# Retention in chunks of 64 tokens instead of 128, with all its products in quarters of TensorE's array

## The chip, the cores and the metric

The kernel runs on one core of one Trainium2 chip. The metric is device time in microseconds (us) for one execution; the time given for a kernel is the median over several runs.

## What is computed

One decoder layer on 2048 tokens of width 1024. One input projection of the normalised x (1024 to 2816 columns) feeds two head groups; both results are gated, put side by side and mapped back by an output projection, and x is added. Group B is a sliding-window attention with 8 heads; the change does not touch it. Group A is retention with 4 heads, keys of 64 and values of 128 columns, cut to its core:

```python
qc, kc, vc = chunks(q), chunks(k), chunks(v)              # chunks of C tokens, N = S / C
decay = where(diff >= 0, exp(log_g * diff), 0)            # diff = i - j inside a chunk
scores = einsum('bhnid,bhnjd->bhnij', qc, kc) * decay
intra = einsum('bhnij,bhnje->bhnie', scores, vc)
zeta = exp(log_g * (C - 1 - i))
kv = einsum('bhnjd,bhnje->nbhde', kc * zeta, vc)
state = exp(log_g * C) * state + kv                       # one step for each chunk; prev is the state before it
cross = einsum('bhnid,nbhde->bhnie', qc * xi, prev)       # xi = exp(log_g * (i + 1))
ro = intra + cross                                        # then a norm over each head's 128 columns
```

The result is the same for every length of chunk: a longer chunk has more inside it (`intra`) and fewer steps of the state.

## The kernel before

**The large products.** Four products (query and key columns of the attention, of the retention, gates, output projection) hold most of TensorE's time. Each splits its float32 operands into a high and a low part and multiplies those in three passes (fp32r). Each is made of blocks of 2x2 with seven products instead of eight (`Turns`, `products`). In the profile they are the tile `acc` with 128x512 or 128x384 columns. ScalarE makes the high part of every block `x` and `w`, VectorE the low part; VectorE and ScalarE also take the sums out of PSUM.

**The small products.** Transposes, logits, values and retention write PSUM banks, all named `m` in the profile. Logits (`m<-ks,qT`) use the array in eighths (64 rows by 32 columns), the values' products halves and quarters.

**Retention** (`retention`, lines 860 to 1040). It walks over 16 chunks `c` of 128 tokens. For each chunk the DMA queue loads `a` (queries and keys) and `v`; VectorE applies the rotation and makes `qk`; ScalarE scales the keys (line 920); `qk` is transposed by DMA to `qkT`. TensorE then makes, in plain fp32 (two records in the profile for each matmul):

- the scores of all four heads, in quarters of 64x64, and behind them, into the same two banks `pros`, the part of the state (lines 946 to 967; `m<-qkT`, `m<-state,qkT`). The bank is chosen by the half of the array's rows: `pros[i]` with rows `halves[i]`;
- the outputs from the decayed scores `sT` and `v`, in the whole 128x128 array (lines 977 to 989; `m<-v,sT`);
- the update `pkv` from `qk` and `v`, in halves of 128x64 (lines 993 to 1001; `m<-v,qk`).

VectorE multiplies the scores by the decay mask `dm` (two instructions of 128x256 a chunk, line 968) and steps the state (two of 128x128 a chunk, line 1009). ScalarE copies the outputs to `ro` (line 1029). After each four chunks a group norm runs: some twenty small VectorE instructions, 16 normalisations on ScalarE, and stores of `ro` to DRAM, one of 256 KB for each chunk (line 1077). The gate stage loads it back as `go` (line 1403), multiplies by SiLU of the gate and turns it for the output projection: even chunks by DMA, odd chunks on TensorE (`m<-ident,go`).

**What sets the order.** Nothing is ordered by hand. Every operation is put into `Program` with a cost for each engine, what it reads and writes, and a due time in units of large products; `emit` (line 169) then writes one fixed order for each engine. It counts a change of the array's shape on TensorE (`CUTS`, `CHANGE`, line 90) and holds back shapes that would change it. Buffers come from pools: 93 of 2 KB a partition (`k`), 6 half ones (`h`, for `sT` and the state), 8 PSUM banks, of which the small products may hold six (`SHARE`, `rest`). Each engine runs its instructions in this order, so one that waits holds up all behind it. All DMAs but one are issued by the SP queue.

Of the kernel before, what the change touches and what calls it, by code (L numbers as in the profile page):

```python
# [29 lines left out]
F32 = mybir.dt.float32  # L30
# [26 lines left out]
CAP = {"k": 93, "h": 6, "bank": 8}  # L57
# [334 lines left out]
def layer(ctx, tc, xt, xfirst, xtok, nw, w_in, w_rn, qkw, sinks, biasg, rope, decays, dmask, gpow, w_out, out):  # L392
# [40 lines left out]
    def given(ap):  # L433
        return Buf(ap=ap)
# [48 lines left out]
    rsq_all = fixed([P, NCH], "rsq_all")  # L483
    dec = fixed([P, 2, RH], "dec")
# [15 lines left out]
    ro_dram = scratch([P, 512], "ro_dram", NCH)  # L500
# [359 lines left out]
    def retention(at):  # L860

        for i, (t, r) in enumerate(zip(factors, (rstd_all, rsq_all))):
            op(
                {"V": (0.25, 0.33, True)},
                lambda e, t=t, r=r, i=i: e.tensor_tensor(
                    t(), dec()[:, i : i + 1, :].to_broadcast([P, NCH, RH]),
                    r().unsqueeze(2).to_broadcast([P, NCH, RH]), ALU.mult,
                ),
                [dec, r], [t], at(0) - 6, label="factors",
            )  # L870
        op(
            {"V": (0.25, 0.33, True)}, lambda e: e.tensor_tensor(squares(), factors[0](), factors[0](), ALU.mult),
            [factors[0]], [squares], at(0) - 6, label="factors",
        )
        dm = kb("dm", "ret")
        load(dm, given(dmask.rearrange("p h i -> p (h i)")), at(0) - 4)
        state = None
        st = None
        for c in range(NCH):
            due = at(c)  # L880
            a, v = kb("a", "rin"), kb("v", "rin")
            a0, a1 = (Part(a, lambda t, s=s: t[:, s]) for s in (slice(0, 384), slice(384, 512)))
            v0, v1 = (Part(v, lambda t, s=s: t[:, s]) for s in (slice(0, 256), slice(256, 512)))
            soon = due - (EARLIER_K if c in TURNED["qk"] else 0)
            load(a0, rq_dram[0][c], soon - 3, 192, also=(a,))
            load(a1, rq_dram[1][c], soon - 3, 64, also=(a,), of=lambda t: t[:, 0:128])
            if c % NP == 0:
                phases = kb("phases", "rin")
                load(phases, given(rope[c // NP]), soon - 3)
            load(v0, rq_dram[1][c], due - 3, 128, also=(v,), of=lambda t: t[:, 128:384])  # L890
            load(v1, aq_dram[1][c], due - 3, 128, also=(v,), of=lambda t: t[:, 256:512])

            tcos, tsin, qk = kb("tcos", "ret"), kb("tsin", "ret"), kb("qk", "ret")
            for i, t in enumerate((tcos, tsin)):

                def go(e, t=t, a=a, phases=phases, o=c % NP * 64 + i * 32):
                    h = "p (h f) -> p h f"
                    e.tensor_tensor(
                        t().rearrange(h, f=32), a().rearrange(h, f=32),
                        phases()[:, o : o + 32].unsqueeze(1).to_broadcast([P, 16, 32]), ALU.mult,  # L900
                    )

                op(both(512), go, [a0, a1, phases], [t], soon, label="rotary", also=(a,))

            for i, alu in enumerate((ALU.subtract, ALU.add)):

                def go(e, i=i, alu=alu, tcos=tcos, tsin=tsin, qk=qk):
                    r = "p (h a f) -> p h a f"
                    x, y = (tcos, tsin) if i == 0 else (tsin, tcos)
                    e.tensor_tensor(  # L910
                        qk().rearrange("p (a b f) -> p a b f", b=2, f=32)[:, :, i, :],
                        x().rearrange(r, h=2, f=32)[:, 0],
                        y().rearrange(r, h=2, f=32)[:, 1],
                        alu,
                    )

                op(both(256), go, [tcos, tsin], [qk], soon + 0.1, label="rotary sum")


            def go(e, qk=qk, c=c):  # L920
                for h in range(RH):
                    k = qk()[:, 256 + h * RDK : 256 + (h + 1) * RDK]
                    e.activation(k, k, AF.Copy, scale=factors[1]()[:, c, h : h + 1])

            op({"A": (0.95, 1.05, False)}, go, [qk, factors[1]], [qk], soon + 0.15, label="scale k")

            pt, qkT = ps(), kb("qkT", "ret")

            if c in TURNED["qk"]:
                turn_by_dma(qk, qkT, planes_dram[3][c], soon + 0.1)  # L930
            else:

                def go(e, pt=pt, qk=qk):
                    for i in range(4):
                        e.transpose(pt()[:, i * P : (i + 1) * P], qk()[:, i * P : (i + 1) * P], ident())

                op(turns(4), go, [qk, ident], [pt], due + 0.2, "small", label="turn qk")

                op({"A": act(512)}, lambda e, pt=pt, qkT=qkT: e.activation(qkT(), pt(), AF.Copy), [pt], [qkT], due + 0.3,
                   label="qkT")  # L940
            halves = (slice(0, 64), slice(64, 128))


            pros, sTs = [ps(), ps()], [hb("sT"), hb("sT")]

            def go(e, pros=pros, qkT=qkT, state=state):
                for pr in range(2):
                    for u, q in enumerate(halves):
                        for i, r in enumerate(halves):
                            o = 256 + pr * P  # L950
                            e.matmul(
                                pros[i]()[q, o : o + P], qkT()[r, o + u * 64 : o + u * 64 + 64],
                                qkT()[r, pr * P : (pr + 1) * P], start=True, stop=True,
                            )
                for pr in range(2 if state else 0):
                    for u, q in enumerate(halves):
                        for i, r in enumerate(halves):
                            o = pr * P
                            e.matmul(
                                pros[i]()[q, o : o + P], qkT()[r, o + u * 64 : o + u * 64 + 64], state()[r, o : o + P],  # L960
                                start=(pr == 0), stop=False, skip_group_check=True,
                            )

            op(
                f32(P, 2 if c == 0 else 4), go, [qkT] + ([state] if c else []), pros,
                due + 0.4, "quarters", label="scores",
            )
            for i in range(2):
                op(
                    {"V": dve(256)},  # L970
                    lambda e, sT=sTs[i], pro=pros[i], i=i: e.tensor_tensor(
                        sT(), pro()[:, 256:512], dm()[:, i * 256 : (i + 1) * 256], ALU.mult
                    ),
                    [pros[i], dm], [sTs[i]], due + 0.5, label="decay",
                )

            def go(e, pros=pros, sTs=sTs, v=v, c=c):
                for pr in range(2):
                    for i in range(2):
                        h, s = 2 * pr + i, slice(pr * P, (pr + 1) * P)  # L980
                        e.matmul(
                            pros[i]()[:, s], sTs[i]()[:, s], v()[:, h * P : (h + 1) * P], start=(c == 0 and pr == 0),
                            stop=(pr == 1), skip_group_check=True,
                        )

            op(
                f32(P, 4), go, [*sTs, v0, v1], pros, due + 0.6, "small",
                label="outputs", also=(v,),
            )
            if c < NCH - 1:  # L990
                pkv, new = ps(), hb("state")

                def go(e, pkv=pkv, qk=qk, v=v):
                    for h in range(RH):
                        r = slice((h % 2) * 64, (h % 2) * 64 + 64)
                        e.matmul(
                            pkv()[r, (h // 2) * P : (h // 2 + 1) * P], qk()[:, 256 + h * 64 : 256 + (h + 1) * 64],
                            v()[:, h * P : (h + 1) * P], start=True, stop=True,
                        )

                op(f32(P, 2.5), go, [qk, v0, v1], [pkv], due - 1.0, "columns", label="update", also=(v,))
                if c == 0:
                    op(
                        {"V": dve(256)}, lambda e, new=new, pkv=pkv: e.tensor_copy(new(), pkv()[:, 0:256]),
                        [pkv], [new], due + 0.6, label="state",
                    )
                else:
# [22 lines left out]
            if c % NORMED == 0:  # L1030
                st, ros = sb("st", [P, NORMED, RH, 6]), []
# [582 lines left out]
```

## Time and profile before

| What | Value |
|---|---|
| Time, median of 3 runs | 692.14 us (691.63 to 695.44) |
| Span of the profiled execution | 689.9 us, 2.2 us below that median |
| TensorE busy | 683.8 us, 99% of the span |
| VectorE busy | 602.1 us, 87% |
| ScalarE busy | 474.1 us, 69% |
| GpSimd busy | 46.1 us, 7% |
| Bytes moved by DMA | 179.16 MB, mean 260 GB/s |

The profile is of one execution; its span runs from the first to the last instruction. In it PE is TensorE's matmuls, PEld its weight loads, DVE VectorE, ACT ScalarE, POOL GpSimd, SPq the queue that issues DMAs. A row such as `m<-v,sT 128*128 128x128 f32 x128` reads: written tile, read tiles, part of the array in use (rows*columns), size of the moving operand, type, count. A busy time is a union of records that overlap, so the time of one instruction in a row of equals is read from start to start. All of the kernel's instructions have one line, that of the helper that records them, so tiles tell them apart.

### The profile page before, as it was taken

To read this page: it belongs to the slowest core of one execution; us is meant where nothing else is said; L and a number is where in the kernel's file an instruction comes from. 1 tells how busy PE (TensorE), PEld (TensorE's weight loads), DVE (VectorE), ACT (ScalarE), POOL (GpSimd) and SP (SyncE) were. 2 spreads that over 40 slices of the span, in tenths; PEclk is the share of its full clock that TensorE was granted. 3 is DMA by queue.
4 is the path that set the end of the run, shared out by engine and by line. 5 is a ranking of instruction groups with operands and counts; after the bars stand their busy time and mean duration, and the time that the engine had idled before them with its cause. 6 is when DMAs were issued, how large, how long until landed. Compare 5 with 4: busy or idle time off the path is not lost.

```text
span 689.9 us, 15034 instructions
## 1 busy us (share of the span) xinstructions
PE 683.8 (99%) x5164; PEld 586.9 (85%) x5164; DVE 602.1 (87%) x1467; ACT 474.1 (69%) x1121; POOL 46.1 (7%) x75
## 2 busy tenths in 40 slices
PE   9999999999999999999999999999999999999998
PEld 7888888889999999997888888888888888888886
DVE  6999887777899978998999989997979899998862
ACT  7666974657796766888868989989789944253300
POOL 1000000035011001012101010100000000000000
PEclk9999999999999999999999999999999999999999
DMA  9999964989987799999999989899999998126622
GB/s 324 363 352 313 386 209 167 337 289 286 325 217 198 219 297 283 314 287 282 325 284 251 328 242 292 248 221 340 273 355 316 228 274 229 32 76 208 221 106 92
DMA packets 166717, 179.16 MB, mean 260 GB/s; under 512 B 71152, under 2 KB 99824, under 8 KB 166640
## 3 DMA queue, kind: packets, MB, share of 16 engines
q1 hardware_dynamic: 166496, 178.19, 86.4%
q8 instruction: 41, 0.67, 0.4%
q14 instruction: 36, 0.29, 0.1%
q10 hardware_dynamic: 144, 0.00, 0.0%
HBM read 106.77 MB, written 56.69 MB: 237 GB/s over the span
## 4 chain that ended last, share of the span: by engine, by line
PE 99%; issue 0%; DVE 0%
PE acc L388 84%; PE m L388 15%; DVE t L388 0%; DVE none L388 0%
## 5 line engine op out<-in xcount | busy, mean ns | idle before, releaser
L388 PE MATMUL acc<-w,x 128*128 128x512 f32 (+1 forms) x2700 | 589.9, 377 | 0.0
L388 PEld LDWEIGHTS acc<-w,x 128*128 128x128 f32 x2700 | 493.1, 188 | 79.9 <-issue 2.3
L388 DVE TENSOR_TENSOR x<-x 128x512 fp32r<-128x512 f32 (+2 forms) x220 | 145.3, 683 | 16.6 <-ACT x L388 16.5
L388 ACT ACTIVATE x<-x 128x512 fp32r<-128x512 f32 (+1 forms) x187 | 110.9, 615 | 17.4 <-DVE x L388 11.7
L388 DVE TENSOR_TENSOR w<-w 128x512 fp32r<-128x512 f32 (+3 forms) x96 | 61.7, 659 | 2.7 <-ACT w L388 2.3
L388 ACT ACTIVATE w<-w 128x512 fp32r<-128x512 f32 (+1 forms) x72 | 40.7, 599 | 21.0 <-DVE w L388 10.2
L388 ACT ACTIVATE pm<-lg,nm 128x128 f32<-128x128 f32 x128 | 49.7, 393 | 5.2 <-DVE lg L388 5.1
L388 DVE TENSOR_TENSOR s<-acc,s 128x512 f32<-128x512 f32 (+1 forms) x64 | 41.6, 651 | 10.9 <-PE acc L388 10.3
L388 DVE SCALAR_TENSOR_TENSOR w<-w,nw_sb 128x512 fp32r<-128x512 f32 (+3 forms) x72 | 49.5, 709 | 1.2 <-ACT w L388 1.1
L388 DVE CUSTOM_DVE_ANT_0 lg<-m,bias,nsnk 128x160 f32<-128x160 f32 x128 | 42.4, 379 | 7.6 <-PE m L388 7.5
L388 POOL TENSOR_SCALAR_AFFINE_SELECT own<-pT 64x512 f32<-64x512 f32 x32 | 29.0, 920 | 243.9 <-ACT pT L388 214.2
L388 DVE TENSOR_TENSOR t<-acc,t 128x512 f32<-128x512 f32 (+2 forms) x33 | 21.1, 640 | 17.7 <-PE acc L388 17.1
L388 ACT ACTIVATE x<-go 128x512 fp32r<-128x512 f32 x40 | 24.1, 623 | 13.1 <-PE acc L388 3.5
L388 DVE TENSOR_TENSOR x<-go,x 128x512 fp32r<-128x512 f32 x40 | 27.3, 682 | 2.5 <-ACT x L388 2.5
L388 ACT ACTIVATE apart<-qn 128x1024 uint16<-128x1024 uint16 x16 | 16.9, 1054 | 18.2 <-DVE qn L388 18.1
L388 ACT ACTIVATE w<-w,nw_sb 128x512 fp32r<-128x512 f32 (+3 forms) x43 | 27.5, 677 | 2.6 <-DMA w<-in_w_in 2.6
L388 ACT ACTIVATE s<-acc 128x512 f32<-128x512 f32 (+1 forms) x32 | 18.0, 566 | 14.6 <-PE acc L388 11.7
L388 DVE TENSOR_TENSOR r<-acc,t 128x512 f32<-128x512 f32 (+1 forms) x32 | 20.8, 651 | 7.0 <-PE acc L388 6.7
L388 ACT ACTIVATE ro<-ro,nmu,rg 128x128 f32<-128x128 f32 x64 | 25.1, 481 | 0.4 <-DVE nmu L388 0.4
L388 ACT ACTIVATION_READ_ACCUMULATOR pm<-lg,nm 128x1 f32 x128 | 24.5, 191 | 0.0
L388 ACT ACTIVATE c<-acc 128x512 f32<-128x512 f32 (+1 forms) x24 | 13.3, 560 | 15.1 <-PE acc L388 13.1
L388 PE MATMUL m<-ks,qT 64*32 64x160 f32 x1024 | 22.1, 300 | 1.6 <-issue 1.6
(132 smaller groups left out, 681.7 us busy)
## 6 DMA issues: line engine op xcount, KB each, us to landing
x<-in_xt SPq DMA_DIRECT2D x80, 256.0 KB, 4.8
x<-s_dram SPq DMA_DIRECT2D x64, 256.0 KB, 4.6
planes_dram<-apart SPq DMA_DIRECT2D x56, 256.0 KB, 4.2
w<-in_w_in SPq DMA_DIRECT2D x40, 256.0 KB, 5.4
s_dram<-x SPq DMA_DIRECT2D x32, 256.0 KB, 4.5
xk<-in_xtok SPq DMA_DIRECT2D x32, 256.0 KB, 5.2
res<-in_xtok SPq DMA_DIRECT2D x32, 256.0 KB, 3.8
w<-in_w_out SPq DMA_DIRECT2D x20, 256.0 KB, 5.2
```

Of the source, the lines that this page charges most:

```text
L388: return lambda *a, **k: self.order.put(op(*a, **k))
```

## The change

The chunk of retention becomes 64 tokens. The program takes two old chunks of 128 tokens, four of 64, at a time (`for c in range(0, NCH, 2)`).

- **Update**: eight quarter matmuls for each 128 tokens instead of four in halves, one bank `kvs[u]` for each half `u` of the rows, that is for each chunk of 64 of the two.
- **State**: it is stepped every 64 tokens, 31 times instead of 15; the pool `h` has 8 buffers instead of 6. An update may go only behind the scores of the pair before (`held_up`).
- **State's part, scores, outputs**: state's part goes first, then the scores, 64 columns wide instead of 128, only inside a chunk of 64. Outputs are quarter matmuls as well. A pair of old chunks holds four banks; the bank is `banks[i ^ u][pr]`, where `i` is the head of a pair and `u` the chunk of 64.
- **Places**: a bank then holds, in its two halves of partitions, two heads of different chunks. So `ro` has tokens of one half in the other half of the partitions for some heads. The factors of the norm are laid out to match (`rstd_crossed`, made by two small DMAs), and `ro` goes to DRAM in three stores of 128, 64 and 64 KB for each two heads of two chunks, 48 instead of 16.
- **Decay**: the mask is 128x256 instead of 128x512, and one instruction takes both chunks: 16 instead of 32.
- Keys are loaded and turned earlier (`EARLIER_K` 3.0 instead of 1.0).

```diff
-CAP = {"k": 93, "h": 6, "bank": 8}
+CAP = {"k": 93, "h": 8, "bank": 8}
+HALVES = (slice(0, 64), slice(64, 128))
-EARLIER_Q, EARLIER_K, LATER_W = 2.0, 1.0, -1.0
+EARLIER_Q, EARLIER_K, EARLIER_U, LATER_W = 2.0, 3.0, 0.0, -1.0
...
+    def update(c, chunks, states, due):
+        kvs = [ps(), ps()]
+        steps = [(k, u) for k in range(2) for u in range(2) if 2 * (c + k) + u < 2 * NCH - 1]
+        def go(e):
+            for k, (qk, _, v, _) in enumerate(chunks):
+                for pr in range(2):
+                    for u, r in enumerate(HALVES):
+                        for i, q in enumerate(HALVES):
+                            h, o = 2 * pr + i, (2 * k + pr) * P
+                            if (k, u) in steps:
+                                e.matmul(
+                                    kvs[u]()[q, o : o + P], qk()[r, 256 + h * 64 : 256 + (h + 1) * 64],
+                                    v()[r, h * P : (h + 1) * P], start=True, stop=True, skip_group_check=True,
+                                )
...
+    def retain(c, chunks, states, dm, due, ros):
+        mine = states[2 * c : 2 * c + 4]
+        banks = [[ps() for _ in range(2)] for _ in range(2)]
+        def go(e):
+            for k in (1, 0):
+                qkT = chunks[k][1]
+                for pr in range(2):
+                    for u in range(2):
+                        for i, r in enumerate(HALVES):
+                            o = pr * P + u * 64
+                            if mine[2 * k + u] is not None:
+                                e.matmul(
+                                    banks[i ^ u][pr]()[HALVES[u ^ pr], k * P : (k + 1) * P], qkT()[r, o : o + 64],
+                                    mine[2 * k + u]()[r, pr * P : (pr + 1) * P], start=k == 1, stop=False,
+                                    skip_group_check=True,
+                                )
+            for k, (_, qkT, _, _) in enumerate(chunks):
+                for pr in range(2):
+                    for u, q in enumerate(HALVES):
+                        for i, r in enumerate(HALVES):
+                            o, to = pr * P + u * 64, 256 + (2 * k + pr) * 64
+                            e.matmul(
+                                banks[i ^ u][0]()[q, to : to + 64], qkT()[r, 256 + o : 256 + o + 64],
+                                qkT()[r, o : o + 64], start=False, stop=False, skip_group_check=True,
+                            )
...
+        def go(e):
+            for k, (_, _, v, _) in enumerate(chunks):
+                for x in range(2):
+                    for pr in range(2):
+                        for u, r in enumerate(HALVES):
+                            h, o = 2 * pr + (u ^ x), (2 * k + pr) * 64
+                            e.matmul(
+                                banks[x][pr]()[HALVES[u ^ pr], k * P : (k + 1) * P], sTs[x]()[r, o : o + 64],
+                                v()[r, h * P : (h + 1) * P], start=False, stop=True, skip_group_check=True,
+                            )
...
+            for to, rows, x in ro_parts[c // 2][pr]:
+                def go(e, ro=ro, to=to, rows=rows, x=x):
+                    t = ro()[rows, :].rearrange("p (k x d) -> p k x d", k=2, x=2)
+                    e.dma_start(to(), t if x is None else t[:, :, x, :])
+                op(dma(128 if x is None else 64), go, [ro], [to], due + 0.6, label="store ro")
```

The order is written anew by `emit`. Three places on TensorE show how. In the order's rows, `acc` is a large product, `m<-v,qk` the update, `m<-qkT` the scores, `m<-state,qkT` the state's part, `m<-v,sT` the outputs, `m<-ks,qT` logits and `m<-ident,pm` transposes of the attention; the size is that of what is written, the last number how many follow each other.

First, the middle of retention. Before, TensorE's rows of one chunk:

```order
L388 MATMUL acc<-w,x 128x512 x60
L388 MATMUL m<-v,qk 64x128 x12
L388 MATMUL m<-ks,qT 32x160 x32
L388 MATMUL m<-qkT 64x128 x8
L388 MATMUL m<-state,qkT 64x128 x8
L388 MATMUL acc<-w,x 128x512 x15
L388 MATMUL m<-v,sT 128x128 x4
L388 MATMUL acc<-w,x 128x512 x30
```

Now, the rows of a pair:

```order
L390 MATMUL acc<-w,x 128x512 x24
L390 MATMUL m<-v,qk 64x128 x16
L390 MATMUL m<-ks,qT 32x160 x16
L390 MATMUL acc<-w,x 128x512 x24
L390 MATMUL m<-state,qkT 64x128 x16
L390 MATMUL m<-qkT 64x64 x16
L390 MATMUL acc<-w,x 128x512 x9
L390 MATMUL m<-v,sT 64x128 x16
```

The outputs, which stood among large products of the array's full shape, are now quarters with large products on one side or both; logits go in two halves of 16.

Second, the sixth pair of chunks. Before, the outputs of that part of the program:

```order
L388 MATMUL m<-state,qkT 64x128 x8
L388 MATMUL m<-v,sT 128x128 x8
L388 MATMUL acc<-w,x 128x512 x21
L388 MATMUL m<-v,sT 128x128 x4
L388 MATMUL acc<-w,x 128x512 x84
```

Now:

```order
L390 MATMUL acc<-w,x 128x512 x24
L390 MATMUL m<-ident,pm 128x128 x4
L390 MATMUL m<-state,qkT 64x128 x16
L390 MATMUL m<-qkT 64x64 x16
L390 MATMUL m<-ident,pm 128x128 x4
L390 MATMUL m<-v,sT 64x128 x16
L390 MATMUL m<-v,qk 64x128 x16
```

Between scores and outputs stand four transposes now.

Third, the end of retention, from the last outputs on. Before:

```order
L388 MATMUL m<-v,sT 128x128 x12
L388 MATMUL acc<-w,x 128x512 x69
L388 MATMUL m<-ident,go 128x128 x4
L388 MATMUL acc<-w,x 128x512 x12
L388 MATMUL m<-ident,go 128x128 x4
```

Six more transposes of gated rows follow there. Now:

```order
L390 MATMUL m<-ident,go 128x128 x4
L390 MATMUL acc<-w,x 128x512 x6
L390 MATMUL m<-v,sT 64x128 x16
L390 MATMUL acc<-w,x 128x512 x42
L390 MATMUL m<-ident,go 128x128 x4
L390 MATMUL acc<-w,x 128x512 x12
L390 MATMUL m<-ident,go 128x128 x4
L390 MATMUL acc<-w,x 128x512 x12
L390 MATMUL m<-ident,go 128x128 x4
L390 MATMUL acc<-w,x 128x512 x75
L390 MATMUL m<-ident,go 128x128 x4
L390 MATMUL acc<-w,x 128x512 x9
```

The last outputs, of the last two chunks, stand behind the first three transposes of gated rows instead of ahead of all eight; one more transpose follows the last row shown.

More of the change, by code (lines that the diff above doesn't have):

```diff
@@ L905, in retention @@
[L905 to L917, printed above, removed]
@@ L920, in go @@
[L920 to L940, printed above, removed]
@@ L941, in retention @@
[L941 to L989, printed above, removed]
```

239 lines of the change are left out of this document (155 added, 84 removed).

## Prediction

> **What bounds the kernel now.** I read the page first: its busy times and the chain that ended last.
>
> ```profile
> span 689.9 us, 15034 instructions
> ...
> PE 683.8 (99%) x5164; PEld 586.9 (85%) x5164; DVE 602.1 (87%) x1467; ACT 474.1 (69%) x1121; POOL 46.1 (7%) x75
> ...
> PE 99%; issue 0%; DVE 0%
> PE acc L388 84%; PE m L388 15%; DVE t L388 0%; DVE none L388 0%
> ```
>
> TensorE is never idle and is the whole chain. Its large products (tile `acc`) hold 84% of the span, the small ones into banks named `m` 15%; the change touches a part of these. A microsecond taken from TensorE is a microsecond of the span, as long as the others keep up. So I ask next how near they are, in the stretch where retention runs and the two behind it (columns: stretch, its length, busy time and count for each engine, granted clock, share and rate of the DMA engines).
>
> ```profile
> 310.00:500.00 190.00, 188.33 (x1985) 158.01 (x1984) 175.47 (x536) 163.55 (x403) 14.43 (x14) 1.00 1.01 280
> 500.00:545.00 45.00, 45.00 (x216) 37.33 (x215) 37.07 (x68) 41.87 (x74) 0.00 (x0) 1.00 1.10 319
> 545.00:600.00 55.00, 55.00 (x245) 45.55 (x244) 55.00 (x92) 25.42 (x42) 0.00 (x0) 1.00 0.72 190
> ```
>
> VectorE (third engine) has 92% in retention's stretch and 100% in 545 to 600; ScalarE (fourth) has 93% in 500 to 545. TensorE leads, but not by much. The clock is 1.00 throughout.
>
> The groups by shape give retention's four products. Its fp32 matmuls have two records each; the mean of a record overlaps its neighbours, so only the counts are used.
>
> ```profile
> L388 PE MATMUL m<-v,sT 128*128 128x128 f32 x128 | 16.4, 277 | 0.0
> L388 PE MATMUL m<-qkT 64*64 64x128 f32 x256 | 10.4, 275 | 0.0
> L388 PE MATMUL m<-state,qkT 64*64 64x128 f32 x240 | 9.5, 269 | 0.0
> ...
> L388 PE MATMUL m<-v,qk 128*64 128x128 f32 x120 | 8.3, 279 | 0.0
> ```
>
> The price of a record comes from the timeline of TensorE, from the start of one group to the start of the next.
>
> ```profile
> 340.00 16.59 PE L388 MATMUL acc<-w,x 128*128 128x512 f32 x72
> 356.44 0.27 PE L388 MATMUL m<-ident,kn 128*128 128x128 f32 x1
> ...
> 391.27 1.09 PE L388 MATMUL m<-v,qk 128*64 128x128 f32 x16
> 392.30 1.65 PE L388 MATMUL acc<-w,x 128*128 128x512 f32 x6
> ...
> 476.75 1.53 PE L388 MATMUL m<-v,qk 128*64 128x128 f32 x24
> 478.22 5.78 PE L388 MATMUL acc<-w,x 128*128 128x512 f32 x24
> 483.92 0.67 PE L388 MATMUL m<-qkT 64*64 64x128 f32 x16
> 484.41 0.62 PE L388 MATMUL m<-state,qkT 64*64 64x128 f32 x16
> ...
> 486.16 0.62 PE L388 MATMUL m<-state,qkT 64*64 64x128 f32 x16
> 486.70 0.98 PE L388 MATMUL acc<-w,x 128*128 128x512 f32 x3
> 487.52 2.84 PE L388 MATMUL m<-v,sT 128*128 128x128 f32 x24
> 490.11 2.07 PE L388 MATMUL acc<-w,x 128*128 128x512 f32 x8
> ```
>
> Quarters (64*64): four groups of 16 from 484.41 to 486.16, 1.75 us, 27.3 ns a record. Whole array (v,sT): 2.59 us for 24, 108 ns. Halves (v,qk): 1.03 us for 16 and 1.47 for 24, so 55 ns for each further one. An acc record: 16.44 us for 72, 228 ns.
>
> **The change part by part.** *Outputs* (v,sT): 128 records at 108 ns, 13.8 us, become 256 quarter records at 27.3 ns, 7.0 us: 6.8 us gained. Only the two 64x64 blocks on the diagonal of each old 128x128 operand are left: the block above them was zero, the one below now comes through the state. *Update* (v,qk): 120 at 55 ns, 6.6 us, become 248 quarters, 6.8 us: 0.2 lost. *State's part* (state,qkT): 240 become 248, 0.2 lost.
>
> *Scores* (qkT): still 256 records, but 64 columns wide instead of 128. No row shows that width in quarters. The nearest are the eighths with 160 columns, and the weight loads:
>
> ```profile
> 288.60 0.78 PE L388 MATMUL m<-ks,qT 64*32 64x160 f32 x32
> 289.31 5.50 PE L388 MATMUL acc<-w,x 128*128 128x384 f32 x30
> ...
> 388.06 1.34 PE L388 MATMUL m<-ks,qT 64*32 64x160 f32 x64
> 389.33 0.67 PE L388 MATMUL m<-qkT 64*64 64x128 f32 x16
> ...
> L388 PEld LDWEIGHTS m<-ks,qT 64*32 64x32 f32 x1024 | 16.2, 105 | 5.8 <-issue 5.3 <-PE acc L388 0.3 <-DMA vn<-aq_dram 0.3
> ...
> L388 PEld LDWEIGHTS m<-v,sT 128*128 128x128 f32 x128 | 15.6, 191 | 1.1 <-DVE sT L388 0.4 <-DVE qk L388 0.2
> ...
> L388 PEld LDWEIGHTS m<-qkT 64*64 64x64 f32 x256 | 7.6, 133 | 1.9 <-issue 0.6 <-PE acc L388 0.3 <-ACT c L388 0.3
> ```
>
> Eighths take 0.71 us for 32 records and 1.27 for 64: 17.5 ns for each further one, so each of eight tiles takes 140 ns for 160 columns, and each of four quarters 4 x 27.3 = 109 ns for 128. That is about 1 ns a column, and 64 columns would stream in some 47 ns. A load of 32, 64 and 128 columns takes 105, 133 and 191 ns: some 56 ns for 64 columns on top of a fixed part. At 128 columns the load is hidden (109, not 109 + 56), so I expect 56 ns for a quarter's turn, 14 ns a record, 3.6 us in all against 7.0. Bounds: 3.2 us, and 7.0 if load and stream don't overlap here. I take 3.6, as the rows at 128 columns show the overlap: 3.4 us gained.
>
> The Trainium skill, page "TensorE: Matmul & The Clock Gate", section "Wait — 56ns, not 53.3ns?", says that matmuls never start closer than about 25 ns, however few columns they have. By that rule the scores would take 256 x 25 = 6.4 us. The eighths at 17.5 ns a record stand against it for packed tiles.
>
> Records together: 6.8 + 3.4 - 0.2 - 0.2 = 9.8 us gained.
>
> *Changes of tile shape.* Going into quarters cost 5.70 us for the 24 acc records before 483.92 against 24 x 0.228 = 5.48, and 0.05 in the first group; coming out 0.54 instead of 0.44. That is 0.37 a visit, 0.185 a change. Counted over all of TensorE's order, neighbours of unlike shape go from 66 to 86: outputs used to run in the whole array like acc and now each is a visit of its own, and the logits (`ks,qT`) stand in two halves more often, since a pair of chunks holds four of the six banks that small products share. 20 x 0.185 = 3.7 us lost. Outputs behind acc paid 0.13 too (0.82 us before 487.52 for three acc), six times, 0.8 us, which goes. Net 2.9 lost; bounds 0 (if the drain hides among shorter groups) and 3.7. TensorE's work falls by 9.8 - 2.9 = 6.9 us.
>
> *New waits on TensorE.* VectorE stands between scores and outputs, and between update and state's part.
>
> ```profile
> L388 DVE TENSOR_TENSOR sT<-m,dm 128x256 f32<-128x256 f32 x32 | 12.1, 413 | 0.1
> ...
> L388 DVE SCALAR_TENSOR_TENSOR state<-state,gp,m 128x128 f32<-128x128 f32 x28 | 8.3, 337 | 0.0
> ```
>
> Four states of two instructions (8 x 0.337 = 2.7 us) follow each update; the shortest cover in the new order is 12 acc and the values products, over 5 us. The two decays (0.83 us) between scores and outputs have from 1.4 us of cover up, except at one place (the second one shown of the order), where only four transposes, some 0.4 us, stand between them: 0.4 us late or, with a hand-over, 0.9; I take 0.7. What queues behind a waiting decay on VectorE are splits of `x`, which have buffers ahead.
>
> One idle stretch of TensorE is left in the sum, since nothing that the change touches ends it:
>
> ```profile
> 318.32 1.24 PE L388 MATMUL m<-ks,qT 64*32 64x160 f32 x50 [1.64 <-issue]
> ```
>
> It lies inside one group and waits for nothing that the profile shows. If it doesn't come again, 1.6 us more are gained; another one costs as much.
>
> *The end of retention.* In the order before, 225 acc records stand between the last outputs and the last transposes of gated rows (`ident,go`); now 150, of which 141 stand ahead of the seventh transpose and nine more ahead of the eighth. 141 x 0.228 = 32.2 us and 1.1 for three transposes are 33.3; the eighth 35.7. What lies between shows in the old timelines of ScalarE and the DMA queue and in the list of DMA issues:
>
> ```profile
> 507.04 6.27 ACT L388 ACTIVATE ro<-ro,nmu,rg 128x128 f32<-128x128 f32 x16
> ...
> 519.53 0.53 SPq L388 DMA_DIRECT2D go<-ro_dram  x1
> ...
> go<-ro_dram SPq DMA_DIRECT2D x16, 256.0 KB, 5.3
> ```
>
> From the outputs' end at 490.1 to the last load's landing at 519.5 + 5.3 = 524.8 are 34.7 us, and some 0.7 for the gate's multiplication: 35.4. What was covered by 51 us is now covered by 35.7. The stores of `ro` become 48 instead of 16, so three issues follow the last normalisation instead of one, about 1 us more. I take 1.0 us of waiting; bounds 0 and 4.
>
> *At nothing:* keys are loaded 2 due units earlier and two more half buffers hold states; ScalarE does as many copies and normalisations of the same size; the two small DMAs that cross `rstd` and the three multiplications of factors come long before; the smaller mask saves a part of one load.
>
> Sum: 6.9 - 0.7 - 1.0 = 5.2 us. The profiled span of 689.9 becomes 684.7; the median of the runs shown is 2.2 us above that span, so 692.1 becomes 686.9, say 687.0.
>
> **The rivals.** *VectorE takes it back.* State adds 32 x 0.337 = 10.8 us, the decays drop 16 x 0.413 = 6.6: 4.2 more. In 310 to 545 it has 212.5 busy of 235; it would have 216.7. If the 92.4% of 310 to 500 is its limit there, the stretch needs 216.7 / 0.924 = 234.5 us, and 0.5 us is left: 691.6. For it: it is full from 545 to 600. Against: it waits for TensorE's results too, which come sooner. 0.20.
>
> *Narrow scores gain nothing*, because load and stream of a quarter don't overlap at 64 columns: 3.4 us less, 690.3. Against: the overlap at 128. 0.08. By the floor of 25 ns in the Trainium skill (the page and section above) it would be 2.8 us less, 689.7.
>
> *Changes of shape cost little*: their 3.7 us go, 683.2. Against: each visit in the timeline pays. 0.10.
>
> *Slower: banks shared between row halves.* Before, every bank that quarters write gets its partial sums from one half of the array's rows (`pros[i]` by row half `i`). Now scores, state's part and outputs write bank `i ^ u`: two quarters on the diagonal, of unlike row halves, write one bank at once, in different partitions. If these take turns, two quarters run instead of four and 248 and 256 records at 27.3 ns and 256 at 14 double: 6.8 + 7.0 + 3.6 = 17.4 us, and 692.1 - 5.2 + 17.4 = 704.3. The kernel is slower than before from 30% of that on. No row of before shows such a pair. The Trainium skill, "TensorEngine Tiling (Array Packing)", section "Restrictions and Gotchas", states that different row tiles cannot access the same PSUM bank simultaneously; by that rule this is what happens. Against: the two write different partitions, and update keeps one bank to a row half in any case. 0.08.
>
> **How the numbers follow.** A measurement of this kernel can tell about 0.5%, 3.5 us, so faster is below 688.7 and slower above 695.6. The forecast has 0.54. Faster: the forecast without the 0.05 that its own waits (up to 4.9 instead of 1.7) carry past 688.7, and cheap changes: 0.49 + 0.10 = 0.59. Same: that 0.05, VectorE's 0.20 without the 0.02 in which it overshoots, and the scores' 0.08: 0.31. Slower: banks and that 0.02: 0.10. The range runs from cheap changes, 683, to past VectorE's 691.6, 692.5; it leaves out the banks and a little at both ends.
>
> **What would show it.** In the new profile: quarter records of 27 ns in outputs and update and 14 ns in the scores, by the same timeline; 0.2 us at each change of shape; one late decay; TensorE's idle time before the last two transposes of gated rows. The bank rival shows as 55 ns a record in state's part with update still at 27. If TensorE's busy share falls below 98% with waits for VectorE, that rival has won. The forecast is wrong if TensorE's time outside these four products moves by more than the 2.9 us of changes.

## The result and the profile after

| | before | after |
|---|---|---|
| Time, median | 692.2 us (691.63 to 695.44, 4 runs) | 711.4 us (707.95 to 713.38, 4 runs) |
| Span of the profiled execution | 689.9 us | 711.6 us |
| TensorE busy | 683.8 us, 99% | 687.2 us, 97% |

The changed kernel is slower: the ratio is 1.0265 (95% interval 1.0225 to 1.0304). Every execution counted here is an undisturbed one, and a ratio can differ from that of the two medians by up to some 0.15%. The page of the changed kernel, its busy times and its last chain:

```profile
span 711.6 us, 15589 instructions
...
PE 687.2 (97%) x5428; PEld 580.3 (82%) x5428; DVE 605.7 (85%) x1483; ACT 474.1 (67%) x1122; POOL 42.7 (6%) x75
...
PE 28%; DVE 6%; DMA 5%; ACT 3%; SPq 2%; issue 1%; DVEq 0%; ACTq 0%
```

TensorE was 99% of the chain; now the chain leaves it again and again. (It could be followed back only to 380.9 us, the last 46% of the span, so its shares add up to 45% and not to 100%.) What TensorE waits for (total, times, longest), in the changed kernel:

```profile
PE m L390 <- ACT ro L390: 6.2, 2, 4.3
PE acc L390 <- ACT s L390: 3.8, 3, 2.0
PE m L390 <- DVE sT L390: 3.5, 2, 2.9
PE acc L390 <- DVE x L390: 2.2, 3, 1.2
PE acc L390 <- DVE w L390: 1.4, 1, 1.4
...
PE m L390 <- DVE go L390: 1.0, 1, 1.0
```

With the four others these are 21.2 us; the same view of before has 2.9. TensorE's timeline at the longest of them:

```profile
402.06 0.77 PE L390 MATMUL m<-ks,qT 64*32 64x160 f32 x32
404.67 1.36 PE L390 MATMUL m<-v,qk 64*64 64x128 f32 x32 [1.84 <-ACT ro L390]
410.36 0.48 PE L390 MATMUL m<-ident,kn 128*128 128x128 f32 x1 [4.33 <-ACT ro L390]
```

ScalarE copies a pair's outputs to `ro` and so frees its banks. In ScalarE's timeline the second copy waits for a buffer of the pool, which an earlier store of `apart` (keys split for the turn by DMA) still holds:

```profile
404.26 0.63 ACT L390 ACTIVATE ro<-m 128x256 f32<-128x256 f32 x2
409.92 0.66 ACT L390 ACTIVATE ro<-m 128x256 f32<-128x256 f32 x2 [5.04 <-DMA planes_dram<-apart]
```

And that store was issued late. The timeline of SP's queue:

```profile
392.95 1.99 SPq L390 DMA_DIRECT2D ro_dram<-ro  x3
395.04 0.54 SPq L390 DMA_DIRECT2D x<-s_dram  x1
395.68 6.67 SPq L390 DMA_DIRECT2D ro_dram<-ro  x9
402.45 0.54 SPq L390 DMA_DIRECT2D v<-rq_dram  x1
...
405.01 0.36 SPq L390 DMA_DIRECT2D planes_dram<-apart  x1
```

Twelve stores of `ro`, the first group norm's, hold the queue for 8.7 us; loads and the store of `apart` stand behind them. The stores, by the view of their tile (min/median/max ns of SP's queue), before and after:

```profile
L388 SPq DMA_DIRECT2D ro_dram<-ro x16: 319/382/1247, 386.2 to 513.3; - x16
```

```profile
L390 SPq DMA_DIRECT2D ro_dram<-ro x48: 574/605/1649, 393.0 to 559.0; - x48
```

A store of 64 rows takes SP longer (0.605 us) than one of 128 rows (0.382), and there are three times as many. Summed over the timeline's stretches they hold SP for 33.1 us, against 9.4 before; the issues themselves are 30.8 and 7.1 of that.

Each wait also costs behind itself. Busy times and granted clock (the fraction ahead of the last two columns, DMA share and GB/s) in stretches of 3.41 us, the step in which the clock changes in the trace:

```profile
399.08:402.49 3.41, 3.41 (x64) 2.34 (x70) 2.31 (x7) 2.37 (x6) 0.00 (x0) 1.00 0.57 113
402.49:405.91 3.42, 1.58 (x56) 1.07 (x36) 3.42 (x9) 2.40 (x8) 0.00 (x0) 1.00 0.73 203
405.91:409.32 3.41, 0.12 (x4) 0.00 (x0) 0.69 (x5) 0.00 (x0) 0.00 (x0) 0.50 0.96 285
409.32:412.73 3.41, 2.37 (x6) 1.93 (x7) 2.39 (x14) 2.81 (x8) 0.00 (x0) 0.50 0.88 272
412.73:416.16 3.43, 3.43 (x9) 2.64 (x8) 0.71 (x4) 3.01 (x12) 0.00 (x0) 0.50 1.04 263
416.16:419.50 3.34, 3.34 (x20) 2.80 (x19) 3.27 (x9) 1.61 (x4) 0.72 (x1) 1.00 0.99 325
```

During the burst the DMA engines fall to 113 GB/s while SP issues little but stores of 64 and 128 KB. After TensorE has idled, its clock is 0.50 for three stretches, in which it does 5.9 us of work at half speed: 3 us lost. Two more such stretches, at 351.3 and 528.8 us, with TensorE busy throughout, cost 1.7 each.

### The profile page after: what moved, and what is told of

It is laid out like the page before. It is cut to its first block, busy times and chain, and to the rows that moved or that the text cites. A ratio compares the mean times of both kernels' runs of the same rounds, so it can differ in the third digit from the quotient of the medians.

```text
span 711.6 us, 15589 instructions
## 1 busy us (share of the span) xinstructions
PE 687.2 (97%) x5428; PEld 580.3 (82%) x5428; DVE 605.7 (85%) x1483; ACT 474.1 (67%) x1122; POOL 42.7 (6%) x75
## 5 line engine op out<-in xcount | busy, mean ns | idle before, releaser
L390 PE MATMUL acc<-w,x 128*128 128x512 f32 (+1 forms) x2700 | 598.9, 380 | 8.2 <-ACT s L390 3.8
L390 POOL TENSOR_SCALAR_AFFINE_SELECT own<-pT 64x512 f32<-64x512 f32 x32 | 25.6, 813 | 266.2 <-ACT pT L390 218.8
L390 DVE TENSOR_TENSOR t<-acc,t 128x512 f32<-128x512 f32 (+2 forms) x33 | 21.2, 641 | 18.8 <-PE acc L390 18.2
L390 ACT ACTIVATE c<-acc 128x512 f32<-128x512 f32 (+1 forms) x24 | 13.4, 559 | 19.2 <-PE acc L390 16.5
L390 DVE TENSOR_TENSOR t<-acc,s 128x512 f32<-128x512 f32 (+1 forms) x32 | 20.7, 648 | 4.2 <-PE acc L390 4.1
L390 ACT ACTIVATE xk<-xk 128x512 f32<-128x512 f32 x32 | 19.8, 620 | 5.5 <-DMA xk<-in_xtok 5.5
```

The source lines that it names most:

```text
L390: return lambda *a, **k: self.order.put(op(*a, **k))
```

## The experiments

**Theory A**: the 48 narrow stores hold SP's queue in bursts of twelve; what is queued behind comes late, TensorE waits, its clock drops. **Rival B**: VectorE's added state steps. **Rival D**: keys made two units earlier, and two chunks at a time, crowd buffers and transfers. "Replanned" means that the order was written anew; otherwise TensorE, VectorE and ScalarE keep theirs.

**1. One whole store for three.**

```diff
-e.dma_start(to(), t if x is None else t[:, :, x, :])
+if x is None:
+    e.dma_start(ro_rows[c + pr], ro())
```

> The changed kernel, in its own planned order, with one store of 128 rows and 256 KB for each normalised buffer in place of three of 64 rows: 16 stores instead of 48, all on SP's queue, at the place of the first of the three. Half of the output rows land where they don't belong, so the output is not the reference's; the work is otherwise the same. Theory A (the 48 narrow stores take 29 us of SP's queue in bursts of twelve, and the loads and the other stores queued behind them make TensorE wait and its clock drop): 688 to 697 us, the drop of the clock near 400 us gone and ScalarE's waits for the turned buffers shorter. Rival B (VectorE's 31 state steps and later decays): the stores don't matter, 708 to 713. Rival D (the keys' work two units earlier and two chunks at a time crowds the buffers that the loads and stores use): 706 to 713, with the waits before 390 us, where no store has been issued, all still there in any case.

696.8 us, ratio to before 1.0066 (1.0043 to 1.0088): 14.6 of the 19.2 us are gone. A holds; B and D don't explain it.

**2. The 48 stores from GpSimd's queue.**

```diff
-e.dma_start(to(), t if x is None else t[:, :, x, :])
+G.dma_start(to(), t if x is None else t[:, :, x, :])
```

> The changed kernel, in its own planned order, with the 48 stores issued from GpSimd's queue instead of SP's; nothing else differs, and the output is the reference's. Theory A: SP's queue is free of them, 690 to 700 us unless GpSimd issues so slowly that the gate's loads come too late for the output's last products (then up to 705). Rivals B and D: 708 to 713.

696.2 us, 1.0063 (1.0041 to 1.0084). The burst now stands on GpSimd (first row), and SP goes on with its loads:

```profile
391.89 7.21 POOL L390 DMA_DIRECT2D ro_dram<-ro  x12 [19.24 <-ACT ro L390]
```

```profile
391.93 0.54 SPq L390 DMA_DIRECT2D x<-s_dram  x1
392.56 0.38 SPq L390 DMA_DIRECT2D v<-rq_dram  x1
392.99 0.42 SPq L390 DMA_DIRECT2D v<-aq_dram  x1
```

The Trainium skill, page "DMA: Bandwidth & Descriptors", section "Issuing engines are not separate DMA queues", says that issuing from several engines saves only the time to start a DMA, usually small beside the DMA itself. Here the move was worth 15 us: not only the time of the issues, but what stood behind them.

**3. The kernel before with its stores cut in three.**

```diff
-store(ro_dram[c], ro, due + 0.6)
+to, t = (z.rearrange("p (k x d) -> p k x d", k=2, x=2) for z in (ro_dram[c](), ro()))
+e.dma_start(to[0:64], t[0:64])
+for x in range(2):
+    e.dma_start(to[64:128, :, x, :], t[64:128, :, x, :])
```

> The kernel before, in its own planned order, with each of its 16 stores of normalised values cut into three of the shapes that the changed kernel has (64 rows of 1 KB pieces, twice 64 rows of 512-byte pieces) on SP's queue; the planner doesn't know of it and the output is the reference's. Theory A, if the stores are enough by themselves: 701 to 712 us. If they hurt only together with the pairs (a pair's chunks wait for one another): 693 to 698. Rivals B and D: 692, no change.

705.0 us, 1.0181 (1.0143 to 1.0219): the cut alone costs 13.0 us, without pairs, quarters or early keys.

**4. Keys late, stores still on SP** (`EARLIER_K` 1.0 instead of 3.0, replanned).

> The changed kernel with the keys loaded and turned as late as in the kernel before (one due unit ahead instead of three), replanned with that; the output is the reference's. Rival D (keys made early hold buffers that others wait for): 694 to 703 us, the waits at 325 to 349 and 378 us shorter. Theory A: the stores' bursts are still there, 705 to 714. Rival B: 708 to 713.

705.7 us, 1.0188 (1.0154 to 1.0222): 5.7 us less, at the lower end of A's range and above D's. The early keys, or the plan, have a part of their own.

**5 and 6. Stores on GpSimd and keys one or two units ahead** (edit 2 with `EARLIER_K` 1.0 and 2.0).

> The changed kernel with its 48 stores on GpSimd's queue and the keys one due unit ahead instead of three, replanned with that; the output is the reference's. With the stores alone moved it took 696.2 us, of which about 8 are waits at 326 to 350 and 402 us and one stretch of half clock behind them. Theory A+D (those waits are the early keys' turned copies, which crowd the buffers and the transfers before any store): 687 to 692 us. A alone (the rest isn't the early keys): 695 to 700. Rival B (VectorE's state steps make the rest): 695 to 698.

> As the run with the keys one unit ahead and the stores on GpSimd's queue, but with the keys two units ahead. Theory A+D: between the two, 688 to 695 us. If a new plan moves the waits about by chance, and not by how early the keys are, then its waits lie at other places and the time may be on either side of the others by some 3 us.

694.5 us, 1.0040 (1.0024 to 1.0057), and 695.2, 1.0036 (1.0014 to 1.0058). A+D expected more of run 5, and A alone a little less: with the stores gone, later keys bring 1 to 2 us.

**7. One state step in place of two** (edit 2, in its order).

```diff
-for pr in range(2):
-    e.scalar_tensor_tensor(new()[:, s], old()[:, s], gp()[:, pr : pr + 1], kv()[:, o : o + P], ...)
+e.scalar_tensor_tensor(new(), old(), gp()[:, 0:1], kv()[:, 2 * k * P : 2 * (k + 1) * P], ...)
```

> The changed kernel in its own planned order with the 48 stores on GpSimd's queue, and each state step made by one VectorE instruction of 256 columns in place of two of 128. The second pair's heads then get the first pair's decay, so the output is not the reference's. By VectorE's pitch in the trace of before (258 ns for 128 columns, 334 for 256) this takes 31 x (2 x 258 - 334) = 5.6 us from VectorE. Rival B: 690 to 693 us, against 696.2 with both instructions. Theories A and D: 694.5 to 697, since VectorE's work there is not what TensorE waits for.

695.5 us, 1.0055 (1.0035 to 1.0075), against 696.2. VectorE lost 3.4 us of work rather than 5.6, by the groups of the run with the stores on GpSimd and of this one:

```profile
L390 DVE SCALAR_TENSOR_TENSOR state<-state,gp,m 128x128 f32<-128x128 f32 x60 | 17.6, 339 | 0.4 <-PE m L390 0.3
```

```profile
L390 DVE SCALAR_TENSOR_TENSOR state<-state,gp,m 128x256 f32<-128x256 f32 x30 | 14.2, 472 | 0.5 <-PE m L390 0.3
```

Rival B would have shown most of that.

**8. The planner told the price** (`dma(..., 0.65)` for the stores, on SP, replanned).

> The changed kernel with its 48 stores on SP's queue, replanned with 0.65 us of SP's queue for each store instead of 0.45, about what the trace shows (0.605); the output is the reference's. Theory A, if the planner's too small price is what makes the bursts hurt: 694 to 702 us. If the queue itself is too full at that place, whatever the order: 704 to 712. Rivals B and D: 708 to 713.

716.0 us, 1.0354 (1.0297 to 1.0411): outside every expectation. Each of the four bursts is now one piece of twelve, 7.9 to 9.0 us long; in the changed kernel that holds for one of them. SP's queue and TensorE in this run:

```profile
542.78 7.85 SPq L390 DMA_DIRECT2D ro_dram<-ro  x12
550.80 0.96 SPq L390 DMA_DIRECT2D go<-ro_dram  x2
551.80 0.43 SPq L390 DMA_DIRECT2D planes_dram<-apart  x1
```

```profile
589.68 4.24 PE L390 MATMUL acc<-w,x 128*128 128x512 f32 x18
601.78 2.74 PE L390 MATMUL acc<-w,x 128*128 128x512 f32 x5 [7.86 <-ACT x L390]
```

So telling the planner the price of one issue doesn't help: it puts all twelve together. The longest wait, 7.9 us, ends 51 us behind the last burst, and the chain to it runs through VectorE and a load of weights; that the bursts cause it isn't shown, and a part of this run's loss may be its plan.

**9. As 5, with one state step.**

> As the run with the stores on GpSimd's queue and the keys one unit ahead (694.5 us, where the chain goes through VectorE alone from 568 to 600 us), in that run's order, with each state step one VectorE instruction of 256 columns instead of two of 128: 5.6 us less of VectorE's work, the second pair's heads decayed by the first pair's factor, so the output is not the reference's. If VectorE is the bound once the stores are off SP's queue and the keys are late (rival B, second in line): 689 to 692 us. If the waits at 575 to 600 us come of the order and not of VectorE's load: 693.5 to 696.

694.9 us, 1.0036 (1.0011 to 1.0060): no gain, though the chain of run 5 goes through VectorE almost alone from 568 to 600 us. B falls again.

**10. The kernel before with early keys** (`EARLIER_K` 3.0, replanned).

> The kernel before with the keys three due units ahead instead of one, replanned with that; the output is the reference's. Rival D (early keys crowd the buffers by themselves): 695 to 700 us. If early keys hurt only with the pairs of chunks: 690 to 694. It also shows how far a new plan alone moves the kernel before.

699.2 us, 1.0088 (1.0055 to 1.0121): 6.6 us slower by medians. Two waits of TensorE that before doesn't have, in its timeline:

```profile
338.64 6.66 PE L388 MATMUL acc<-w,x 128*128 128x512 f32 x21 [1.88 <-DVE x L388]
...
390.03 0.66 PE L388 MATMUL m<-v,qk 128*64 128x128 f32 x8 [4.11 <-issue]
```

**11 and 12. As 5, with one more buffer, or with values and state one unit earlier** (`CAP` 94 and 7; `EARLIER_U` 1.0; replanned).

> As the run with the stores on GpSimd's queue and the keys one unit ahead (694.5 us), with one more of the 2-KB buffers (94 instead of 93) and one fewer of the half buffers (7 instead of 8), replanned with that; the output is the reference's. If the remaining waits come of too few buffers: 690 to 693 us. If they move about with each new plan: anywhere from 691 to 698, at other places.

> As the run with the stores on GpSimd's queue and the keys one unit ahead (694.5 us), with the values loaded and the two states of a pair updated one due unit earlier, replanned with that; the output is the reference's. If the waits at 372 to 376 us (the next pair's update waits for the copies of the last outputs) come of the update falling due with its own outputs: 691 to 693.5 us. If not: 694 to 698.

696.8 us, 1.0057 (1.0036 to 1.0079), and 697.5, 1.0064 (1.0031 to 1.0096): neither helps.

**13. The kernel before with less work for TensorE** (outputs of chunks past the first for one pair of heads only).

```diff
-for pr in range(2):
+for pr in range(1 if c else 2):
```

> The kernel before in its own order, with 60 of the 128 records of TensorE's outputs left out (the second pair's heads in every chunk but the first get the state's part alone, so the output is not the reference's). That takes 60 x 108.4 ns = 6.5 us from TensorE and changes nothing on any other engine or queue. If time taken from TensorE's records comes through when the order stays (the gain was lost to the new order): 685.0 to 687 us. If the other engines and transfers take it back whatever the order, as a kernel at 99% of TensorE that has no slack left: 689.5 to 692.

688.5 us, 0.9964 (0.9937 to 0.9990): between the two. Some 6.5 us leave TensorE and 3.4 come through (0.7 to 4.4 by the ratio). In its trace TensorE is busy for 678.5 us, 5.3 less than before and not 6.5, and runs into waits that before didn't have (4.2 us in all against 2.9), as here:

```profile
359.53 1.48 PE L388 MATMUL m<-v,sT 128*128 128x128 f32 x8 [0.44 <-DVE sT L388]
...
368.93 0.55 PE L388 MATMUL m<-qkT 64*64 64x128 f32 x11 [0.62 <-DVE nm L388]
```

**14 and 15. Stores on GpSimd, keys 0 and 1.5 units ahead** (replanned).

> The changed kernel with its 48 stores on GpSimd's queue and the keys not ahead at all (0 due units; 3 took 696.2, 2 took 695.2, 1 took 694.5 us), replanned; the output is the reference's. If earlier keys cost by a steady rate: 693 to 694.5 us. If the turned keys now come late, or if each new plan has its own waits: 695 to 700, with waits for the turned keys in the retention.

> The same with the keys 1.5 due units ahead, replanned; the output is the reference's. If the waits follow how early the keys are: 694 to 695.5 us, as its two neighbours. If they follow the single plan: 691 to 699, with waits at places that neither neighbour has.

Without a lead 694.3 us, 1.0038 (1.0016 to 1.0060), with 1.5 units 699.5, 1.0107 (1.0078 to 1.0137). At 1.5 it is slower than at 1 and at 2, and just above the wider of the two ranges: beyond a small trend the single plan decides.

**16 and 17. Stores almost without bytes, short packets without more issues.** In 16 the first store is whole and the two others write one number of each row (first diff); in 17 one store writes four pieces of 512 B a row (second).

```diff
+else:
+    e.dma_start(ro_rows[c : c + 2, 64:128, pr * 256 : pr * 256 + 1].rearrange("k t d -> t k d"), t[:, :, x, 0:1])
```

```diff
+if x is None:
+    apart = ro_rows[c + pr].rearrange("(j q) (r d) -> j (q r) d", j=4, d=P)
+    e.dma_start(apart.rearrange("j p d -> p j d"), ro().rearrange("p (j d) -> p j d", j=4))
```

> The changed kernel in its own order; of each three stores the first is one whole store of 128 rows (2-KB packets) and the other two store only one number of each of 64 rows, so SP still issues 48 stores in the same bursts while the DMA engines have almost nothing more to do than with 16 whole ones. Output rows land where they don't belong, so the output is not the reference's. Theory A (SP's queue): 705 to 712 us. If the short packets on the full DMA engines are what hurts: 695 to 698, as with 16 whole stores (696.8).

> The changed kernel in its own order with one store of 128 rows for each buffer, each row cut into four pieces of 512 B that land apart: 16 issues on SP, with four times the packets of 16 whole stores. Output rows land where they don't belong, so the output is not the reference's. Theory A (SP's queue): 696 to 699 us. If the short packets are what hurts: 704 to 712.

Run 16: 760.7 us, 1.0984 (1.0942 to 1.1026); run 17: 695.0, 1.0038 (1.0021 to 1.0055). Short packets cost nothing that shows. Run 16 lies far above both its ranges, for a reason of its own. Its SP queue, and the row on its stores in the view of what SP waits for (total, times, longest):

```profile
392.14 5.18 SPq L390 DMA_DIRECT2D ro_dram<-ro  x3
397.42 0.77 SPq L390 DMA_DIRECT2D x<-s_dram  x1
399.04 15.24 SPq L390 DMA_DIRECT2D ro_dram<-ro  x9
414.33 0.83 SPq L390 DMA_DIRECT2D v<-rq_dram  x1
```

```profile
SPq L390 <- DMA ro_dram<-ro: 57.5, 39, 3.3
```

A store there takes SP no longer than a real one (0.58 us for the tiny ones), but SP waits for an earlier store to land, mostly before it issues the next one, 57.5 us in all; the changed kernel has no such row. The likely reason, not tried by itself, is that the stores of this run write the same rows of DRAM. So run 16 shows what it costs when SP's queue stands, and doesn't separate issues from bytes.

Summed over the timeline, the stores hold SP, issuing or waiting, for 14.1 us in run 1, 15.2 in run 17, 33.1 in the changed kernel and 84.6 in run 16, for 696.8, 695.0, 711.4 and 760.7 us, all in one order of the engines. Runs 1 and 17 differ by no more than their spread; from them to the changed kernel, and from it to run 16, each us of the queue goes with 0.8 to 1.0 us of time.

**18. As 13, with lighter transfers.**

```diff
-load(o, (ro_dram, so_dram)[n][c], due - 4)
+e.dma_start(o()[:, 0:256], src()[:, 0:256])
+G.memset(o()[:, 256:512], 0.0)
```

> The kernel before in its own order, with TensorE's 60 records of outputs left out as in the earlier run (688.5 us, of 6.5 us only half came through), and besides the 32 loads of the gate's operand from DRAM halved to 128 KB (GpSimd writes zeros over the other half; the output is not the reference's): 4.2 MB less for the DMA engines from 405 to 640 us. If full DMA engines took the other half back: 685 to 686.5 us. If it was lost to waits between the engines, or before 405 us: 687.5 to 689.5.

688.6 us, 0.9954 (0.9929 to 0.9978), as without the edit. Full DMA engines are not what took run 13's other half, at least from 405 us on.

## Why the prediction was wrong

**Inside their groups the records came as priced.** TensorE's timeline of the changed kernel, a pair without waits and the end of the sixth:

```profile
428.23 1.10 PE L390 MATMUL m<-state,qkT 64*64 64x128 f32 x32
429.16 0.64 PE L390 MATMUL m<-qkT 64*64 64x64 f32 x32
429.73 0.78 PE L390 MATMUL m<-ks,qT 64*32 64x160 f32 x32
...
431.33 1.10 PE L390 MATMUL m<-v,sT 64*64 64x128 f32 x32
432.37 9.82 PE L390 MATMUL acc<-w,x 128*128 128x512 f32 x42
...
459.86 0.66 PE L390 MATMUL m<-ident,pm 128*128 128x128 f32 x4
460.48 1.22 PE L390 MATMUL m<-v,sT 64*64 64x128 f32 x32
461.51 1.05 PE L390 MATMUL m<-v,qk 64*64 64x128 f32 x32
462.50 3.01 PE L390 MATMUL acc<-w,x 128*128 128x512 f32 x12
```

From start to start, state's part takes 0.93 us, scores 0.57, outputs 1.04, update 0.99, each with the way out of its group. Against 32 x 27.3 ns = 0.87 and 32 x 14 = 0.45, the ways out take 0.06 to 0.17. The rival of shared banks would have doubled state's part; it takes 29 ns a record with the way out, and the rule of the Trainium skill, "TensorEngine Tiling (Array Packing)", section "Restrictions and Gotchas", that different row tiles can't use one bank at the same time, cost nothing here where the two write different partitions. That narrow scores gain nothing fell too: with the way out a record takes 18 ns, below the 25 that the Trainium skill gives in "TensorE: Matmul & The Clock Gate", section "Wait — 56ns, not 53.3ns?". That holds by the record, as the prediction counted; a matmul has two of them here, and so 36 ns.

**TensorE's work as a whole fell by about half of what was summed.** The sum had 9.8 us less for records and 2.9 more for changes of shape, 6.9 net. TensorE's busy time went from 683.8 to 687.2 us, of which 6.4 are half speed (3 and twice 1.7): 680.8, so 3.0 less. Runs 6 and 14, whose clock never drops, have 679.9 and 681.3, 3.9 and 2.5 less. Counted over the trace from start to start, with waits and half speed taken out, the four products take 8.2 us less with their ways out, and all else on TensorE takes 5.2 more, 4.5 of that in the large records of 512 columns. So the sign that the prediction gave for being wrong, more than 2.9 us outside the four products, is there. The changes are as many as it counted (66 and 86); what else lengthens the large records, short stalls or the ends of groups in front of a wait, stays open. With this the spans add up: 18.3 us more of waits and 6.4 of half speed, less 3.0, are the 21.7 between 689.9 and 711.6.

**The step that failed** is "The stores of `ro` become 48 instead of 16, so three issues follow the last normalisation instead of one, about 1 us more". It looked at the last of four group norms only, and there at three issues. At each of the four, twelve issues stand on SP's queue nearly in a row, in front of loads and of the stores of `apart`, and that is the term that was mis-sized: 1 us expected, 15 to 16 measured (runs 1, 2 and 17), and 13.0 in the kernel before (run 3). At the one place that the term looked at it was right: TensorE waits 1.0 us for gated rows (`go`). The issue time of a 64-row store, 0.605 us, had no row in before; the sum's 1 us for two more issues is 0.5 each. The late decay of the sixth pair, where 0.7 us was expected, cost 0.2: outputs start 0.62 us after its four transposes, which take 0.44 elsewhere. The longest wait for a decay, 2.9 us, stands at the last outputs, and with the stores moved (run 2) the longest is 0.7.

**"At nothing"** stood the earlier keys. In the kernel before they cost 6.6 us, new plan included (run 10), and with the stores on SP later keys gain 5.7 (run 4). With the stores moved they matter by 2 us (runs 2, 5, 6, 14), no more than what plans differ by (run 15).

**"A microsecond taken from TensorE is a microsecond of the span, as long as the others keep up"**: they don't quite. Run 13 changes nothing but TensorE's work, and about half comes through, with a wide interval.

**The clock** was in no term. A wait of 2 us can cost 1.7 more, which is how waits grow into a loss beyond their own length.

**VectorE's rival** said that a busy share below 98% with waits for VectorE would show it. The share is 97%, and `sT` and `x` stand among the waits; but cutting VectorE's work had no effect (runs 7 and 9). The sign was badly chosen, since a late transfer shows as a wait for whichever engine uses it.

**Still open**: the changed kernel with its stores on GpSimd stays 2.3 to 7.6 us above before in seven versions (runs 2, 5, 6, 11, 12, 14, 15), though its records are shorter. Each plan has a few waits of 1 to 3 us at places of its own, and these take back the small gain: in run 14 TensorE waits 7.2 us against 2.9 before and has 2.5 less work. Neither VectorE's load, one more buffer, nor (in the kernel before) lighter transfers explains them; that pairs hold four banks at once wasn't tried by itself. No version here that does all of the work beats the kernel before.

## What to carry to other kernels

When a change cuts a transfer into pieces, count the pieces on the queue that issues them, at every place where they are issued and not only at the last, and name what stands behind them there. A new layout that leaves TensorE shorter pays only if its results can still leave in as few issues, or from a queue on which nothing urgent stands; here even that only brought it back to 2 to 8 us above before. Where TensorE is busy to 99%, treat each new wait of 2 us as up to 4, and a gain in records as about half, as in these runs.

## What the runs showed of the hardware

- **The clock drops after less idle time than one thinks.** Counted over all these traces in stretches of 3.41 us: each stretch with 1.9 us or more of idle TensorE was followed by one at half clock, none with under 1.3 us was, and between them both happened. It came back behind a stretch with 0.3 us idle or less. The Trainium skill, "TensorE: Matmul & The Clock Gate", section "Part 1: The HAM clock gate (the "warmup" mystery)", has the same 3413 ns and speaks of an idle window; here a window that was idle for little more than half was always enough.
- **SP's time for a store goes by its shape, not its bytes** (medians): 0.382 us for 128 rows of 2 KB (before), 0.42 for 128 rows in pieces of 512 B (run 17), but 0.58 to 0.61 for 64 rows in two pieces each, whether these have 1 KB, 512 B (changed kernel) or 4 B (run 16).
- **Twelve such issues in a row starve the DMA engines**: 113 to 203 GB/s in and behind the burst, 325 later.
